# Spatial products of a gating group's two blocks, issued together in the down products' PSUM pool

## The chip, the cores and the metric

The kernel runs on one core of one Trainium2 chip. Its time is the device time of one execution in microseconds (us); the figure is the median of three runs. The core has five engines that work side by side, each on its own queue in order: TensorE (PE, matmuls; PEld is its weight load), VectorE (DVE), ScalarE (ACT), GpSimd (POOL, unused here) and SyncE (SP, which issues the DMAs). Matmul results land in PSUM banks, from which DVE and ACT read them. Engines wait for each other by semaphores.

## What is computed

One step of a two-layer streaming encoder for 1024 prompt frames and 32 sample frames, which share weights. Layer 0 has a spatial gating mixer (`sgu_mixer`), layer 1 a pooling mixer; each is followed by a squared-ReLU channel MLP, with RMSNorms and conditioning between. The part that the change touches is this:

```python
def sgu_mixer(h, w_in, g_v, w_s, b_s, w_out, T):
    z = jax.nn.gelu(h @ w_in)
    u, v = jnp.split(z, 2, axis=-1)
    v = rmsnorm(v, g_v)
    vr = v.reshape(bsz, L // T, T, SGU_GROUPS, SGU_GROUP_DIM)
    w = w_s[:, :T, :T] * sgu_chunk_mask()[:T, :T].astype(w_s.dtype)
    s = jnp.einsum('gij,bnjgd->bnigd', w, vr)
    s = s + jnp.transpose(b_s[:, :T])[None, None, :, :, None]
    s = s.reshape(bsz, L, D_SGU)
    return (u * s) @ w_out, v
```

The width is 1024, `u` and `v` are 2048 wide in 8 groups of 256, and T is 128 for the prompt and 32 for the sample.

## The kernel before

**Tiles and products.** The 1056 frames stand as columns in three tiles, `TILES` (L27): 384, 384, and 256 prompt plus 32 sample columns (288). Feature blocks of 128 stand on the partitions. A large product is done in three matmuls per weight block, as both operands are split into a high and a low fp32r part: `products` (L766) issues high·high (L771), high·low (L772) and low·high (L773). Splitting a weight costs one ACT copy (`wh`, L367) and one DVE subtraction (`wl`); splitting an activation costs the same two steps (`split`, ACT L925 and DVE). DVE instructions issued through the planner's wrappers all carry line L79 and are told apart by their tiles.

**The mixer's stages.** First `v` is computed for all frames and written to DRAM (`vd`). Then the loop at the end of the mixer runs over four pairs of groups, (0,1) to (6,7), and within a pair over the three tiles; each step is one `sgu_item`. An item has four blocks, two groups × two 128-wide halves k. For each block before the change `up(g, k)` does:
- if k is 0, `inputs(g)`: DMA of `vl` (the group's rows of `vd`, L968 and L973, on SP's queue) and DVE's scaling of the spatial weights by the frames' norms, `wr`;
- 24 matmuls into `pu`, and ACT's Gelu to `u` (L993);
- the spatial product `psp`: one plain fp32 matmul per 128-frame chunk (L997; each shows as two records), and a small one for the sample frames (L1005);
- DVE: s = psp·g_v + b, then s·u; `split` into `ush` and `usl`.

`down` then forms the item's share of `h = (u·s) @ w_out`: eight output blocks d, each 12 matmuls into `po` over the four pairs `ush`/`usl`, and adds each to the residual accumulator `acc` (ACT for the first pair of groups, DVE after that). `down` is put in `pending` and run by `flush()` of the next item, after that item's first `up`.

**Buffers.** PSUM has 8 banks, in three pools (L136 to L143): `pu` with 2, taken in turn by `ps_up`; `pd` with 3, by `ps_dn`; `pm` with 3, by `ps_ms`. SBUF work tiles come from tag "m" with 3 buffers (`t_m`: `u`, `s`, `wr`, some norm tiles) and tag "c" with 3 (`t_c`). A buffer's next user waits until its last user's readers are done.

**What sets the order.** The program is written out in order, and a planner adds work from other chains. `tick` (L69) advances a model time of PE, DVE calls advance a model time of DVE, and `weave` (L585) pulls a step from `fillers` (residual and modulation chains, conditioning products) whenever DVE's model time is behind PE's, each not before its `gates` time. The framework then fixes each engine's order at build from its own estimate. `weave` also takes steps of one stream of DRAM loads (issued on SP's queue into a few `raw` buffers, L359), which splits the weights and forms the conditioning products `ada` (L453) from DVE's sums `aa` of `w_ada`. In the mixer's first item these `ada` products stand among the matmuls, and a filler writes the sample state's rows: `vst` is loaded (L896), scaled on DVE and written out (L909), all on SP's queue, among which the `vl` loads stand. At the mixer's end, `to_ffn0` puts each tile's residual and modulation chain (`residual`, `modulate`: norms `pn`, `q`, `r`, eight `acc` updates, then `hh` on ACT and `hl` on DVE) into the fillers; the FFN's first products `pf` read `hh` and `hl` of tile 0.

Of the kernel before, what the change touches and what calls it, by code (L numbers as in the profile page):

```python
# [12 lines left out]
ALU = mybir.AluOpType  # L13
AX = mybir.AxisListType

P = 128
# [18 lines left out]
def tile_stream_encoder_step(  # L35
# [27 lines left out]
    mm = nc.tensor.matmul  # L63
# [5 lines left out]
    def tick(us):  # L69
        time["pe"] += us  # L70
        time["dve"] = max(time["dve"], time["pe"] - 4.0)

    def on_dve(op, fixed, rate):
        def run(out, *args, **kw):
            n = 1
            for k in out.shape[1:]:
                n *= k
            time["dve"] += fixed + n / rate
            return op(out, *args, **kw)  # L79

        return run

    tt = on_dve(nc.vector.tensor_tensor, 0.16, 930.0)
    stt = on_dve(nc.vector.scalar_tensor_tensor, 0.16, 840.0)
# [51 lines left out]
    def ps_up(name):  # L136
        return psum.tile([P, 512], F32, tag="pu", bufs=2, name=name)

    def ps_dn(name):
        return psum.tile([P, 512], F32, tag="pd", bufs=3, name=name)  # L140
# [4 lines left out]
    def t_m(name):  # L145
        return work.tile([P, 384], F32, tag="m", bufs=3, name=name)

    def t_c(name):
        return work.tile([P, 384], F32, tag="c", bufs=3, name=name)
# [4 lines left out]
    def t_x(name, shape):  # L154
        return work.tile(shape, F32, tag="x3", bufs=3, name=name)
# [16 lines left out]
    for i, parts in enumerate(rows):  # L172
        n = sum(k for _, k in parts)
# [25 lines left out]
    gvT = vecs[2][:, 24:40]  # L199
# [280 lines left out]
    def run_deferred():  # L480
        for _ in range(len(deferred)):
            deferred.pop(0)()
# [25 lines left out]
    def stream_ready():  # L508
        k = state["next"]
        if k >= len(stream):  # L510
            return False
        if stream[k][0] == "w":
            i = wpos[stream[k][1]] - W_SLOTS // 2
            return i < 0 or worder[i] in wdone
        return True

    def stream_step():

        k = state["next"]
        kind, key, ap, shape = stream[k]  # L520
        issue()
        run_deferred()
        r = raws.pop(k)
        if kind == "w":
            do_w(key, r)
        elif kind == "ada":
            (do_ada_pe if k < first_ada else do_ada)(*key, r)
        else:
            do_x(key, r)
        state["next"] += 1  # L530
        if in_raw(k):
            state["raw"] -= 1
        issue()
# [24 lines left out]
    def pull(force=False):  # L558

        def open_(f):
            return force or gates.get(f[0], 0.0) <= time["pe"]

        if sticky:
            f = sticky[-1]
            if not open_(f):
                return False
            sticky.pop()
        else:  # L570
            f = next((f for f in list(fillers)[:2] if open_(f)), None)
            if f is None:
                return False
        try:
            step = next(f[1])
        except StopIteration:
            fillers.remove(f)
            return True
        if step is True:
            sticky.append(f)  # L580
        elif step is not False:
            gates[f[0]] = max(time["pe"], time["dve"]) + step
        return True

    def weave(streams=1):  # L585
        if streams:
            n = 0
            run_deferred()
            while n < streams and stream_ready():
                stream_step()  # L590
                n += 1
        while time["dve"] < time["pe"] and fillers:
            if not pull():
                break
# [326 lines left out]
    def t_hid(kind, name):  # L921
        return work.tile([P, 384], F32R, tag="h" + kind, bufs=5, name=name)

    def split(dst_hi, dst_lo, src, n):
        act(out=dst_hi[:, :n], in_=src[:, :n], func=AF.Copy)  # L925
        tt(out=dst_lo[:, :n], in0=src[:, :n], in1=dst_hi[:, :n].bitcast(F32), op=ALU.subtract)
# [31 lines left out]
    def sgu_item(gs, t, mix, after):  # L958
        n = ncol[t]
        col0, npr, nsm = TILES[t]  # L960
        nch = npr // P
        hid = []
        vls, wrs = {}, {}

        def inputs(g):
            wt, _ = mix[g]
            vl = vls[g] = t_x(f"vl{g}_{t}", [P, 3, 256])
            nc.sync.dma_start(  # L968
                vl[:, :nch, :],
                vd[col0 : col0 + npr, g * 256 : (g + 1) * 256].rearrange("(c p) d -> p c d", p=P),  # L970
            )
            if nsm:
                nc.sync.dma_start(  # L973
                    vl[:nsm, nch, :], vd[SEQ : SEQ + nsm, g * 256 : (g + 1) * 256]
                )
            wr = wrs[g] = t_m(f"wr{g}_{t}")
            for c in range(nch):
                b = col0 // P + c
                ts(wr[:, c * P : (c + 1) * P], wt, rv[:, b : b + 1], None, op0=ALU.mult)
            if nsm:  # L980
                ts(wr[:nsm, npr : npr + nsm], wt[:nsm, :nsm], rv[:nsm, 8:9], None, op0=ALU.mult)

        def up(g, k):
            f = 2 * g + k
            if k == 0:
                inputs(g)
            vl, wr, bb = vls[g], wrs[g], mix[g][1]
            ps = ps_up(f"pu{g}_{t}_{k}")
            products(ps, n, up_terms(("u", g, k), t))
            if t == NT - 1:  # L990
                w_finish(("u", g, k))
            u = t_m(f"u{g}_{t}_{k}")
            act(out=u[:, :n], in_=ps[:, :n], func=AF.Gelu_apprx_tanh)  # L993
            sp = ps_up(f"psp{g}_{t}_{k}")
            tick(0.24 * nch + 0.2)
            for c in range(nch):
                mm(  # L997
                    sp[:, c * P : (c + 1) * P],
                    vl[:, c, k * P : (k + 1) * P],
                    wr[:, c * P : (c + 1) * P],  # L1000
                    start=True,
                    stop=True,
                )
            if nsm:
                mm(  # L1005
                    sp[:, npr : npr + nsm],
                    vl[:nsm, nch, k * P : (k + 1) * P],
                    wr[:nsm, npr : npr + nsm],
                    start=True,
                    stop=True,  # L1010
                )
            s = t_m(f"s{g}_{t}_{k}")
            stt(
                out=s[:, :npr].rearrange("p (c j) -> p c j", j=P),
                in0=sp[:, :npr].rearrange("p (c j) -> p c j", j=P),
                scalar=gvT[:, f : f + 1],
                in1=bb.unsqueeze(1).broadcast_to([P, nch, P]),
                op0=ALU.mult,
                op1=ALU.add,
            )  # L1020
            if nsm:
                stt(
                    out=s[:, npr : npr + nsm],
                    in0=sp[:, npr : npr + nsm],
                    scalar=gvT[:, f : f + 1],
                    in1=bb[:, :nsm],
                    op0=ALU.mult,
                    op1=ALU.add,
                )
            tt(out=s[:, :n], in0=s[:, :n], in1=u[:, :n], op=ALU.mult)  # L1030
            a, b = t_hid("h", f"ush{g}_{t}_{k}"), t_hid("l", f"usl{g}_{t}_{k}")
            split(a, b, s, n)
            hid.append((a, b))

        def down():
            for d in range(KB):
                ps = ps_dn(f"po{gs[0]}_{t}_{d}")
                terms = []
                for j, (a, b) in enumerate(hid):
                    wh, wl = need_w(("o", gs[j // 2], d // 4))  # L1040
                    o = (j % 2) * 512 + (d % 4) * P
                    terms.append((wh[:, o : o + P], wl[:, o : o + P], a[:, :n], b[:, :n]))
                products(ps, n, terms)
                accumulate(t, d, ps, gs[0] == 0)
                if d == 0 and after is not None:
                    st = Stat(t, f"rs_{t}")
                if after is not None:
                    st.square(d)
                if t == NT - 1 and d % 4 == 3:
                    for g in gs:  # L1050
                        w_finish(("o", g, d // 4))
                weave(d % 2)
            if after is not None:
                after(st)

        for j in range(4):
            up(gs[j // 2], j % 2)
            weave()
            if j == 0:
                flush()  # L1060
        pending.append(down)
# [102 lines left out]
    for gs in groups:  # L1164
        mix = {g: sgu_group(g) for g in gs}
# [281 lines left out]
```

## Time and profile before

| | |
|---|---|
| median of three runs | 2240.0 us (2239.03 to 2240.32) |
| profiled execution | 2238.69 us |
| its span in the profile | 2236.9 us |
| mean granted TensorE clock | 0.992 |
| mixer's items, from the first `pu` to the FFN's first `pf` | about 244 to 682 us |
| `pu` products | 384 matmuls of each kind, in 48 blocks |
| `psp` products | 48 blocks |

A profile row of the timeline reads: start, duration, engine, line, operation, out<-in, shape, count, and in brackets the idle time before it with what ended it. Matmuls are pipelined, so the pitch from one start to the next is what one costs, not its duration. A wait row reads: engine, tile and line, what it waited for, total us, times, longest. A row of a stretch gives busy time of PE, PEld, DVE, ACT and POOL with counts, then the granted clock, the DMA engines' share and GB/s.

### The profile page before, as it was taken

The page shows a single profiled execution, that of the slowest core. Times are in us where ns is not written, and L with a number is a line of the kernel's source. Part 1 is how long each engine was busy: PE and PEld are TensorE (multiplying, and loading weights), DVE is VectorE, ACT ScalarE, POOL GpSimd, SP SyncE. Part 2 cuts the span into 40 slices and gives each one's busy share as a digit, 9 for nine tenths or more (in the row PEclk, how much of TensorE's full clock was granted, in tenths as well). Part 3 has the DMA queues.
Part 4 walks back from the last instruction along what each step waited for, and adds up shares of the span by engine and source line. Part 5 has one row for each costly group of instructions (what it writes and reads, how often), then busy time and mean ns, then how long its engine had stood idle before and what let it go on. Part 6 is the DMA issues. An engine that isn't in the chain of part 4 may idle for free.

```text
span 2236.9 us, 33683 instructions
## 1 busy us (share of the span) xinstructions
PE 2197.3 (98%) x13478; PEld 2101.8 (94%) x13478; DVE 1371.4 (61%) x2609; ACT 957.5 (43%) x1645; POOL 0.7 (0%) x6
## 2 busy tenths in 40 slices
PE   7999799999999999999999999999999999999998
PEld 5777699999998999999999999999999999999998
DVE  4855735675568765766446869878765553424355
ACT  4633323121256654133435556666565542312334
POOL 0000000000000000000000000000000000000000
PEclk9999999999999999999999999999999999999998
DMA  8465613232235544333444546665454551202112
GB/s 298 149 226 164 206 53 116 79 126 88 78 104 184 171 132 142 104 123 109 132 125 131 166 156 201 184 189 163 145 166 135 152 155 45 93 10 85 57 50 95
DMA packets 344896, 295.67 MB, mean 132 GB/s; under 512 B 10178, under 2 KB 322954, under 8 KB 344740
## 3 DMA queue, kind: packets, MB, share of 16 engines
q1 hardware_dynamic: 344468, 293.43, 42.1%
q8 instruction: 105, 1.72, 0.3%
q14 instruction: 51, 0.42, 0.1%
q10 hardware_dynamic: 272, 0.10, 0.0%
HBM read 261.65 MB, written 31.84 MB: 131 GB/s over the span
## 4 chain that ended last, share of the span: by engine, by line
PE 91%; DMA 1%; DVE 1%; ACT 1%; issue 0%; DVEq 0%; SPq 0%; ACTq 0%
PE pf L771 11%; PE pf L772 11%; PE pf L773 11%; PE pg L771 11%; PE pg L772 11%; PE pg L773 11%; PE pu L771 3%; PE po L771 3%; PE po L772 3%; PE po L773 3%; PE pu L772 3%; PE pu L773 3%; PE pv L798 1%; PE pv L799 1%; PE pv L800 1%; PE pp L1310 1%
## 5 line engine op out<-in xcount | busy, mean ns | idle before, releaser
L771 PE MATMUL pf<-hh,wh_up 128*128 128x384 f32 (+1 forms) x1536 | 498.0, 324 | 1.2 <-ACT r L1075 1.0
L772 PE MATMUL pf<-hl,wh_up 128*128 128x384 f32 (+1 forms) x1536 | 497.0, 324 | 1.8 <-DVE hl L79 1.7
L771 PE MATMUL pg<-fh,wh_dn 128*128 128x384 f32 (+1 forms) x1536 | 498.3, 325 | 0.0
L773 PE MATMUL pf<-hh,wl_up 128*128 128x384 f32 (+1 forms) x1536 | 496.1, 323 | 0.0
L772 PE MATMUL pg<-fl,wh_dn 128*128 128x384 f32 (+1 forms) x1536 | 494.7, 322 | 0.0
L773 PE MATMUL pg<-fh,wl_dn 128*128 128x384 f32 (+1 forms) x1536 | 494.0, 322 | 0.0
L771 PEld LDWEIGHTS pf<-hh,wh_up 128*128 128x128 f32 x1536 | 288.6, 188 | 4.3 <-issue 2.0
L772 PEld LDWEIGHTS pf<-hl,wh_up 128*128 128x128 f32 x1536 | 288.7, 188 | 3.0 <-DVE hl L79 2.6
L771 PEld LDWEIGHTS pg<-fh,wh_dn 128*128 128x128 f32 x1536 | 288.4, 188 | 3.0 <-issue 1.2
L772 PEld LDWEIGHTS pg<-fl,wh_dn 128*128 128x128 f32 x1536 | 288.6, 188 | 0.7
L773 PEld LDWEIGHTS pg<-fh,wl_dn 128*128 128x128 f32 x1536 | 288.7, 188 | 0.0
L773 PEld LDWEIGHTS pf<-hh,wl_up 128*128 128x128 f32 x1536 | 288.6, 188 | 0.0
L367 ACT ACTIVATE wh_up<-raw 128x1024 fp32r<-128x1024 f32 x144 | 152.7, 1061 | 287.2 <-PE pf L772 230.8
L79 DVE TENSOR_TENSOR wl_up<-raw,wh_up 128x1024 fp32r<-128x1024 f32 x144 | 176.2, 1224 | 160.8 <-ACT wh_up L367 160.4
L79 DVE TENSOR_TENSOR acc<-acc,pg 128x384 f32<-128x384 f32 (+1 forms) x336 | 174.1, 519 | 159.8 <-PE pg L773 159.2
L367 ACT ACTIVATE wh_dn<-raw 128x1024 fp32r<-128x1024 f32 x144 | 152.7, 1061 | 206.2 <-PE pg L772 173.3
L79 DVE SCALAR_TENSOR_TENSOR aa<-raw,csil,aa 128x256 f32<-128x256 f32 x560 | 231.9, 478 | 2.4 <-DMA raw<-in_w_ada_dram 2.4
L79 DVE TENSOR_TENSOR wl_dn<-raw,wh_dn 128x1024 fp32r<-128x1024 f32 x144 | 176.2, 1224 | 86.4 <-ACT wh_dn L367 86.4
L1075 ACT ACTIVATE r<-pf 128x384 f32<-128x384 f32 (+1 forms) x192 | 86.6, 452 | 216.4 <-PE pf L773 211.6
L79 DVE TENSOR_TENSOR fl<-r,fh 128x384 fp32r<-128x384 f32 (+1 forms) x192 | 100.3, 523 | 115.0 <-ACT fh L925 113.6
L771 PE MATMUL pu<-hh,wh_u 128*128 128x384 f32 (+1 forms) x384 | 127.4, 332 | 0.9 <-DVE rv L874 0.9
L771 PE MATMUL po<-ush,wh_o 128*128 128x384 f32 (+1 forms) x384 | 125.6, 329 | 1.9 <-ACT ush L925 1.5
(254 smaller groups left out, 2904.2 us busy)
## 6 DMA issues: line engine op xcount, KB each, us to landing
raw<-in_ffn_w_up_dram SPq DMA_DIRECT2D x144, 512.0 KB, 4.1
raw<-in_ffn_w_down_dram SPq DMA_DIRECT2D x144, 512.0 KB, 3.4
raw<-in_w_ada_dram SPq DMA_DIRECT2D x96, 512.0 KB, 4.1
raw<-in_sgu_w_in_dram SPq DMA_DIRECT2D x32, 512.0 KB, 4.5
xd<-acc SPq DMA_DIRECT2D x8, 1536.0 KB, 7.4
xo_r<-xd SPq DMA_DIRECT2D x32, 384.0 KB, 3.7
vd<-vt SPq DMA_DIRECT2D x32, 256.0 KB, 2.9
raw<-in_sgu_w_out_dram SPq DMA_DIRECT2D x16, 512.0 KB, 3.8
```

The lines of the kernel that those rows point to most:

```text
L79: return op(out, *args, **kw)
L367: act(out=wh, in_=r, func=AF.Copy)
L771: mm(ps[:, :n], wh, rh, start=i == 0, stop=False)
L772: mm(ps[:, :n], wh, rl, start=False, stop=False)
L773: mm(ps[:, :n], wl, rh, start=False, stop=i == last)
L798: mm(ps[:m, :], a_h, wh[:, o : o + 512], start=k == 0, stop=False)
L799: mm(ps[:m, :], a_h, wl[:, o : o + 512], start=False, stop=False)
L800: mm(ps[:m, :], a_l, wh[:, o : o + 512], start=False, stop=k == KB - 1)
L1075: act(out=r[:, :n], in_=ps[:, :n], func=AF.Relu)
L1310: mm(ps[:, :n], wg[:, k, e * P : (e + 1) * P], A(t, 2 * g + k), start=k == 0, stop=k == 1)
```

## The change

`up` keeps the products and the Gelu and puts `u` in a list. A new `gate(g)`, called after the group's second `up`, issues the spatial products of both blocks behind one another into two banks of `pd`, then runs s, s·u and the split for both. `s` comes from tag "c" instead of "m", and one `tick(0.48 * nch + 0.2)` stands for two of `0.24 * nch + 0.2`. The number of matmuls and of DVE instructions is the same.

```diff
+        us = []
+
         def up(g, k):
-            f = 2 * g + k
             if k == 0:
                 inputs(g)
-            vl, wr, bb = vls[g], wrs[g], mix[g][1]
             ps = ps_up(f"pu{g}_{t}_{k}")
             products(ps, n, up_terms(("u", g, k), t))
             if t == NT - 1:
                 w_finish(("u", g, k))
             u = t_m(f"u{g}_{t}_{k}")
             act(out=u[:, :n], in_=ps[:, :n], func=AF.Gelu_apprx_tanh)
-            sp = ps_up(f"psp{g}_{t}_{k}")
-            tick(0.24 * nch + 0.2)
...
+            us.append(u)
+
+        def gate(g):
+
+            vl, wr, bb = vls[g], wrs[g], mix[g][1]
+            sps = []
+            tick(0.48 * nch + 0.2)
+            for k in range(2):
+                sp = ps_dn(f"psp{g}_{t}_{k}")
+                sps.append(sp)
+                for c in range(nch):
+                    mm(
+                        sp[:, c * P : (c + 1) * P],
+                        vl[:, c, k * P : (k + 1) * P],
+                        wr[:, c * P : (c + 1) * P],
+                        start=True,
+                        stop=True,
+                    )
...
+            for k, sp in enumerate(sps):
+                f = 2 * g + k
+                s = t_c(f"s{g}_{t}_{k}")
                 stt(
...
-            tt(out=s[:, :n], in0=s[:, :n], in1=u[:, :n], op=ALU.mult)
-            a, b = t_hid("h", f"ush{g}_{t}_{k}"), t_hid("l", f"usl{g}_{t}_{k}")
-            split(a, b, s, n)
-            hid.append((a, b))
+                tt(out=s[:, :n], in0=s[:, :n], in1=us.pop(0)[:, :n], op=ALU.mult)
+                a, b = t_hid("h", f"ush{g}_{t}_{k}"), t_hid("l", f"usl{g}_{t}_{k}")
+                split(a, b, s, n)
+                hid.append((a, b))
...
         for j in range(4):
             up(gs[j // 2], j % 2)
+            if j % 2 == 1:
+                gate(gs[j // 2])
             weave()
             if j == 0:
                 flush()
```

More of the change, by code (lines that the diff above doesn't have):

```diff
@@ L993, in up @@
             act(out=u[:, :n], in_=ps[:, :n], func=AF.Gelu_apprx_tanh)
-            sp = ps_up(f"psp{g}_{t}_{k}")
-            tick(0.24 * nch + 0.2)
[L996 to L1021, printed above, removed]
-                stt(
-                    out=s[:, npr : npr + nsm],
-                    in0=sp[:, npr : npr + nsm],
+            us.append(u)
@@ new lines, in gate @@
+        def gate(g):
[13 more added lines that the diff above has]
+                    )
+                if nsm:
+                    mm(
+                        sp[:, npr : npr + nsm],
+                        vl[:nsm, nch, k * P : (k + 1) * P],
+                        wr[:nsm, npr : npr + nsm],
+                        start=True,
+                        stop=True,
+                    )
+            for k, sp in enumerate(sps):
+                f = 2 * g + k
+                s = t_c(f"s{g}_{t}_{k}")
+                stt(
+                    out=s[:, :npr].rearrange("p (c j) -> p c j", j=P),
+                    in0=sp[:, :npr].rearrange("p (c j) -> p c j", j=P),
@@ L1025, in up @@
                     scalar=gvT[:, f : f + 1],
-                    in1=bb[:, :nsm],
+                    in1=bb.unsqueeze(1).broadcast_to([P, nch, P]),
                     op0=ALU.mult,
@@ L1029, in up @@
                 )
-            tt(out=s[:, :n], in0=s[:, :n], in1=u[:, :n], op=ALU.mult)
-            a, b = t_hid("h", f"ush{g}_{t}_{k}"), t_hid("l", f"usl{g}_{t}_{k}")
-            split(a, b, s, n)
-            hid.append((a, b))
+                if nsm:
+                    stt(
+                        out=s[:, npr : npr + nsm],
+                        in0=sp[:, npr : npr + nsm],
+                        scalar=gvT[:, f : f + 1],
+                        in1=bb[:, :nsm],
+                        op0=ALU.mult,
+                        op1=ALU.add,
+                    )
+                tt(out=s[:, :n], in0=s[:, :n], in1=us.pop(0)[:, :n], op=ALU.mult)
+                a, b = t_hid("h", f"ush{g}_{t}_{k}"), t_hid("l", f"usl{g}_{t}_{k}")
+                split(a, b, s, n)
+                hid.append((a, b))
         def down():
```

## The prediction

> **What bounds the kernel now.** I read the page's shares and chain first, then the busy time by stage, then TensorE's waits in the mixer, then the timeline around each wait.
>
> ```profile
> PE 2197.3 (98%) x13478; PEld 2101.8 (94%) x13478; DVE 1371.4 (61%) x2609; ACT 957.5 (43%) x1645; POOL 0.7 (0%) x6
> ...
> PE 91%; DMA 1%; DVE 1%; ACT 1%; issue 0%; DVEq 0%; SPq 0%; ACTq 0%
> ```
>
> TensorE (PE) is busy 98% of the span and is 91% of the chain that ended last. No matmul is added or taken away, so only idle time, half-clock time and switching cost of PE can change. The change touches the mixer, about 244 to 682 us. In the next rows the first columns are stretch, length, and busy PE; behind the counts stands the granted clock (0.97, 1.00, 0.99).
>
> ```profile
> 244.00:400.00 156.00, 144.76 (x913) 139.42 (x908) 88.82 (x210) 45.79 (x80) 0.00 (x0) 0.97 0.40 124
> 400.00:560.00 160.00, 160.00 (x1041) 155.67 (x1041) 98.81 (x236) 28.02 (x49) 0.00 (x0) 1.00 0.31 96
> 560.00:682.00 122.00, 119.40 (x752) 116.61 (x751) 76.91 (x151) 50.82 (x82) 0.00 (x0) 0.99 0.32 97
> ```
>
> PE lacks 11.2 us in the first stretch, nothing in the second, 2.6 us in the third. TensorE's waits over 240 to 690 us name the causes (total, times, longest):
>
> ```profile
> PE psp L997 <- DMA vl<-vd: 5.0, 1, 5.0
> PE ada L453 <- DVE aa L79: 4.6, 1, 4.6
> PE pf L772 <- DVE hl L79: 1.7, 1, 1.7
> PE po L771 <- ACT ush L925: 1.5, 1, 1.5
> ```
>
> Two single waits in the first item make 9.6 us; the others stand at the mixer's end. The steady middle has no wait of note except one that hides as pitch, next.
>
> **The change, part by part.** *(1) Gelu waits.* Tile `pu`'s answer lists, under idle time before its engine:
>
> ```profile
>   ACT u L993: 2.6, 16
> ```
>
> Two buffers of pool `pu` serve `pu` and `psp` in turn, so each `pu` takes the bank of the previous `pu` and waits for its Gelu. PE's timeline shows both kinds of block (start, duration):
>
> ```profile
> 280.88 0.83 PE L997 MATMUL psp<-wr,vl 128*128 128x128 f32 x6
> 281.68 0.44 PE L771 MATMUL pu<-hh,wh_u 128*128 128x384 f32 x1
> ...
> 285.95 0.83 PE L997 MATMUL psp<-wr,vl 128*128 128x128 f32 x6
> 286.53 0.42 PE L771 MATMUL po<-ush,wh_o 128*128 128x384 f32 x1
> 286.79 0.34 PE L772 MATMUL po<-usl,wh_o 128*128 128x384 f32 x1
> 286.96 0.34 PE L773 MATMUL po<-ush,wl_o 128*128 128x384 f32 x1
> ```
>
> From psp to the next product it is 0.80 us before `pu` and 0.58 us before `po`: 0.22 us of waiting, 16 times, 3.5 us; the list above says 2.6. After the change `psp` is in pool `pd`, `pu` alternates with `pu`, and the Gelu of two products ago was done 4 us before. I take 3.0 (2.6 to 3.5).
>
> *(2) Fewer switches.* A lone block of plain fp32 passes costs 0.58 for six passes of about 0.091 us (0.55), and the first matmul behind it holds 0.26 instead of the pitch of 0.17 (286.79 to 286.96): 0.12 us per block. The built program has 24 double blocks for 48 single ones: 24 × 0.12 = 2.8 us. Nothing hides it, since PE is the bound here. If the cost goes with passes and not with blocks, it is 0: I take 2.8 (0 to 2.9).
>
> *(3) The first item.* It is the largest term.
>
> ```profile
> 263.65 0.34 PE L773 MATMUL po<-ush,wl_o 128*128 128x384 f32 x1
> 268.59 1.04 PE L453 MATMUL ada<-aa,pick 128*32 128x128 f32 x8 [4.60 <-DVE aa L79]
> 274.60 1.62 PE L997 MATMUL psp<-wr,vl 128*128 128x128 f32 x6 [4.97 <-DMA vl<-vd]
> ...
> 266.98 0.33 SPq L909 DMA_DIRECT2D out_dram<-vst  x1
> ...
> 270.08 0.38 SPq L968 DMA_DIRECT2D vl<-vd  x1
> ```
>
> PE stops at `ada`, then at group 1's first `psp` until `vl` has landed, 4.5 us after its issue; `vl` stands in SP's queue behind the `vst` output, whose DMA it waits for (its place in that queue stays). In the built program three more `pu` products of 24 × 0.174 = 4.2 us now stand ahead of this pair of waits (group 1's second, and both that were behind the first `psp`), 12.5 us, and 18 `po` matmuls (3.1 us) fall behind it: 9.4 us more work ahead. The DVE instructions that feed `vst` and `aa` are moved too: I walked SP's and DVE's order by the rows' durations and get the issue of `vl` near 272 and its landing near 276.5, 1.9 us later. So 9.4 − 1.9 = 7.5 us less idle; about 1.5 us goes back, since the gate's result is then needed by the `po` matmuls close behind. I take 6.0. Lower bound 2: the queue is later by as much as the work ahead, bar the shorter stretch of half clock; upper bound 9: all 9.4 covered.
>
> *(4) The last item.* Rows of its waits, with start and end:
>
> ```profile
> 650.84 0.29 PE L771 MATMUL pu<-hh,wh_u 128*128 128x288 f32 x1
> ...
> 660.80 1.05 PE L997 MATMUL psp<-wr,vl 128*128 128x128 f32 x4 [0.58 <-DVE wr L79]
> ...
> 663.51 0.44 PE L772 MATMUL po<-usl,wh_o 128*128 128x288 f32 x1
> 663.75 0.44 PE L773 MATMUL po<-ush,wl_o 128*128 128x288 f32 x1
> ...
> 672.49 0.67 PE L771 MATMUL po<-ush,wh_o 128*128 128x288 f32 x3 [1.54 <-ACT ush L925]
> ...
> 682.28 0.34 PE L771 MATMUL pf<-hh,wh_up 128*128 128x384 f32 x1
> ```
>
> 650.84 to 682.28 is 31.4 us for 168 products at 0.131 (22.0), three psp blocks of 1.0 and four small matmuls (0.7): 25.7. So 5.7 us are lost, to 0.58, 1.54 and a half clock (pitch 0.24) in between. After, both `pu` of group 7 stand ahead of its `psp` (so `wr` is ready), and the two stalls become one at the second `ush`/`usl`; with DVE's order (s, s·u, a weight split of 1.2, usl, then the second block's) this comes 0.5 to 0.8 us late. Gain 4.9, less 0.7 for what the remaining gap may throttle: 4.2 (1 to 5).
>
> *(5) The boundary to the FFN: a loss.*
>
> ```profile
> 685.53 0.44 PE L772 MATMUL pf<-hl,wh_up 128*128 128x384 f32 x1 [1.69 <-DVE hl L79]
> ...
> 696.09 0.45 PE L771 MATMUL pf<-hh,wh_up 128*128 128x384 f32 x1 [1.01 <-ACT r L1075]
> ...
> 682.48 0.45 DVE L79 TENSOR_TENSOR acc<-acc,po 128x288 f32<-128x288 f32 x1 [0.35 <-PE po L773]
> ...
> 683.36 1.22 DVE L79 TENSOR_TENSOR wl_dn<-raw,wh_dn 128x1024 fp32r<-128x1024 f32 x1
> ...
> 689.53 0.61 DVE L79 SCALAR_TENSOR_TENSOR acc<-acc,coef,r_r_0x 128x384 f32<-128x384 f32 x1
> 690.06 0.61 DVE L79 SCALAR_TENSOR_TENSOR hl<-acc,mod,hh 128x384 fp32r<-128x384 f32 x1
> ...
> 692.79 0.61 DVE L79 SCALAR_TENSOR_TENSOR hl<-acc,mod,hh 128x384 fp32r<-128x384 f32 x1
> ```
>
> Before, tile 0's modulation (eight acc/hl pairs, alternating at 0.53) runs under the last `po`, so the FFN's first half starts at 682.28 and its second at 696.09, 13.8 us on, of which 48 matmuls at 0.174 are 8.4. In the built program the planner's changed estimate puts that chain behind tile 2's last sums on DVE and ScalarE, after the last `po`. From that `po`, E: acc 0.5, two wl_dn to 2.8, two sums and a scale to 4.7, q and r to 5.9, then sixteen instructions at 0.53 to about 15.0; PE, which follows hl by hl, begins the FFN's second half near E + 17.5. Loss 3.7 without half clock. PE's gaps there are short, but a short gap was followed by a throttled clock before:
>
> ```profile
> 660.00:666.40 6.40, 5.58 (x26) 4.71 (x25) 4.34 (x12) 6.00 (x9) 0.00 (x0) 0.75 0.27 89
> ```
>
> Here idle time of 0.8 us cost a mean clock of 0.75 over 6.4 us, that is 1.6 us at most. In the FFN much of that is hidden in waits for hl, so I add 0.8: −4.5 (−2 to −7, the upper loss with the full 1.6 us and each hl 0.1 us later).
>
> The Trainium skill, "TensorE: Matmul & The Clock Gate", section "HAM oscillation — how this bites in real kernels", gives the abstract rule that gaps matter above about 3.4 us. By that rule the short gaps of parts 4 and 5 would throttle nothing, and the sum would be 1.5 us larger. The row above speaks against it: a far shorter gap came with a clock of 0.75.
>
> *(6) The gate's result in the steady middle: 0.* The two blocks' s, s·u, ush, usl now come together, needed by the first `po` behind the next `pu`.
>
> ```profile
> 276.41 0.60 DVE L79 SCALAR_TENSOR_TENSOR s<-psp,vec,bs 128x384 f32<-128x384 f32 x1
> 277.12 0.56 DVE L79 TENSOR_TENSOR s<-s,u 128x384 f32<-128x384 f32 x1
> 278.27 0.56 DVE L79 TENSOR_TENSOR usl<-s,ush 128x384 fp32r<-128x384 f32 x1 [0.59 <-ACT ush L925]
> ...
> 272.85 3.63 DVE L79 SCALAR_TENSOR_TENSOR aa<-raw,csil,aa 128x256 f32<-128x256 f32 x9
> ```
>
> Six instructions of about 0.5 us and one ScalarE hop: 3.4 us after the gate with DVE free. The cover is 24 `pu` products (4.2 us) and six `po` products of the first group (1.0): 5.2 us, 1.8 spare; one weight split of 1.2 fits. DVE is busy 98.8 of 160 us in this stage, so it holds most times. The waits of the two `psp` on sums of earlier `po` in pool `pd` are covered by the same `pu`. The two ticks made one and `s` in another pool cost no instruction; their effect is the order used above.
>
> **Sum.** −3.0 − 2.8 − 6.0 − 4.2 + 4.5 = −11.5 us. The profiled execution took 2238.69 us (span 2236.9 and 1.8 around it); the runs' median, 2240.0, is 1.3 above it, so I take the change off the median: 2228.5.
>
> **The rivals.** *(a) The first item's wait only moves.* If `vl` and `aa` are later by as much as the work put ahead (DVE is the feeder of both, and `aa` rows of 3.63 us stand in its way), term 3 is 0 to 1 and the sum −5.5: 2234.5. For it: `vl`'s place in the queue is unchanged. Against: DVE has less than 2 us more to do ahead of it.
>
> *(b) Slower: the gate's burst comes late on DVE in most items.* Point of decision: more than 1.8 us of other DVE work ahead of the burst. The `aa` row of 3.63 us would do it: 1.8 us late, in 11 items 20 us, less the 11.5 and with no gain at the tail: about +12, 2252. With one item in two it is break-even near 2239. Against: no `po` wait on usl is seen in the middle of the mixer before, and a single split does not exceed the spare time.
>
> *(c) No change.* The chain at the boundary costs 7 and the first item gives its lower bound of 2, with parts 2 and 4 halfway down: −3.0 − 1.5 − 2.0 − 2.5 + 7.0 = −2.0, 2238. The wait of 1.69 on hl shows that DVE is the feeder there; against it, my walk gives 3.7.
>
> That the change fails to do what it says I hold for out: the built order has both `psp` blocks behind the second `pu` in all 24 gates.
>
> **How the numbers follow.** Forecast 0.53, (a) 0.17, (b) 0.15, (c) 0.15. A measurement of this kernel tells 0.2%, 4.5 us, from no change. Faster: nearly all of the forecast (its own range, from the terms' ends taken together in part, is 2221 to 2237, so 0.49), two thirds of (a), 0.12, and a little of (b)'s milder end, 0.03: 0.64. Within: 0.04 + 0.05 + 0.13 + 0.01: 0.22. Slower: 0.14. The range runs from 2220 (first item at 9, tail at 5) to 2245, which takes in (a), (c) and the break-even side of (b).
>
> **What would show it.** In the changed profile: no idle time ahead of `pu` that ends with the Gelu; psp blocks twice as long and half as many; one wait on `vl` under 4 us instead of 5.0, and `ada`'s 4.6 gone; the last item near 26.5 us from `pu` of group 6's second block; FFN's second half 17 to 19 us after the last `po` instead of 13.8, with waits on hl. Wrong would be: waits of `po` on usl all through 300 to 650 us (rival b), or a first-item stall still near 9 us (rival a).

## The result, and the profile after

| | before | changed |
|---|---|---|
| median of five runs | 2239.65 us (2238.24 to 2240.32) | 2230.30 us (2227.71 to 2231.41) |
| profiled execution | 2238.69 us | 2227.71 us |
| span in the profile | 2236.9 us | 2225.9 us |

The ratio is 0.9958, 95% interval 0.9945 to 0.9971: 9.4 us faster, where 11.5 us were forecast (2228.5, range 2220 to 2245).

TensorE's waits of the changed kernel, 240 to 700 us (total, times, longest), answer to those of before:

```profile
PE pn_rs L671 <- ACT sc_rs L656: 3.8, 1, 3.8
PE psp L1005 <- DMA vl<-vd: 2.7, 1, 2.7
PE pf L771 <- ACT hh L745: 1.8, 1, 1.8
PE wsT L952 <- DMA ws<-in_sgu_w_s_dram: 1.6, 2, 1.1
```

The wait of 4.6 us on `aa` is gone, the one on `vl` is 2.7 for 5.0, and neither `pu` on `rv` nor `po` on `ush` is left. New are 3.8 us of `pn_rs` and 1.8 of `pf` on `hh`, both behind the mixer's last `po`. Between 300 and 640 us only one wait stands, of 1.1 us on `ws`, so the gate's burst on DVE is covered in the steady middle.

Before the mixer nothing is changed, yet the two profiles are 2 us apart there. So the stretches are counted from the last `ada` block ahead of the mixer's first `pu` to the FFN's first `pg`. PE's timeline, before:

```profile
243.85 0.42 PE L453 MATMUL ada<-aa,pick 128*32 128x128 f32 x8
...
708.92 0.34 PE L771 MATMUL pg<-fh,wh_dn 128*128 128x384 f32 x1
```

and after:

```profile
245.84 0.42 PE L453 MATMUL ada<-aa,pick 128*32 128x128 f32 x8
...
697.57 0.34 PE L771 MATMUL pg<-fh,wh_dn 128*128 128x384 f32 x1
```

That is 465.1 us before and 451.7 after, 13.3 us less in this pair; the rest of the span behind it is 1528.0 and 1528.3. The two profiled executions are 11.0 us apart, because the time ahead of the mark is 2.0 us longer in the changed kernel's. That execution is also the fastest of its five, so 13.3 us is at the high end. The same stretch in a second profile of the changed kernel is 452.7. The time ahead of the mark lies between 242.6 and 246.6 us over the profiles of this study, which is why single spans are poor evidence for a microsecond or two here.

**The first item, after.** PE's timeline at the stall, then SP's:

```profile
273.60 0.34 PE L773 MATMUL pu<-hh,wl_u 128*128 128x384 f32 x1
273.87 0.43 PE L453 MATMUL ada<-aa,pick 128*32 128x128 f32 x8
277.03 1.58 PE L1005 MATMUL psp<-wr,vl 128*128 128x128 f32 x12 [2.73 <-DMA vl<-vd]
278.36 0.42 PE L771 MATMUL po<-ush,wh_o 128*128 128x384 f32 x1
```

```profile
269.46 0.33 SPq L909 DMA_DIRECT2D out_dram<-vst  x1
...
272.23 0.38 SPq L359 DMA_DIRECT2D raw<-in_w_ada_dram  x1
272.67 0.50 SPq L968 DMA_DIRECT2D vl<-vd  x1
```

Four `pu` now run ahead of `ada`, which finds `aa` ready. `vl` lands 277.03 − 245.84 = 31.2 us after the mark (before: 274.60 − 243.85 = 30.8). Until then PE has three `pu` more to do (12.5 us) and 18 `po` less (3.1 us), so 9.4 us more work. `vl` is issued right behind a load of `w_ada` that stands ahead of it in SP's queue and that had waited 1.9 us for DVE's sums `aa`.

Six `pu` and the first item's 96 `po` are done when the next `psp` starts, before:

```profile
304.33 0.83 PE L997 MATMUL psp<-wr,vl 128*128 128x128 f32 x6
```

and after:

```profile
295.27 1.50 PE L1005 MATMUL psp<-wr,vl 128*128 128x128 f32 x12
```

From the mark that is 60.5 us before and 49.4 after.

**The last item and the boundary, after.**

```profile
639.76 0.29 PE L771 MATMUL pu<-hh,wh_u 128*128 128x288 f32 x1
...
667.10 0.29 PE L773 MATMUL po<-ush,wl_o 128*128 128x288 f32 x1
671.14 0.61 PE L671 MATMUL pn_rs<-sc_rs,ones 128*128 128x288 f32 x1 [3.75 <-ACT sc_rs L656]
671.69 0.61 PE L671 MATMUL pn_rs<-sm_rs,ones 128*128 128x288 f32 x1
674.05 0.69 PE L771 MATMUL pf<-hh,wh_up 128*128 128x384 f32 x1 [1.75 <-ACT hh L745]
...
684.98 0.45 PE L771 MATMUL pf<-hh,wh_up 128*128 128x384 f32 x1 [0.29 <-ACT r L1087]
```

From group 6's second `pu` to the last `po`'s end (667.23) are 27.5 us, one psp block of about 0.9 more than before, against 31.4: 4.9 us gained. The FFN's second half starts 17.75 us after that, against 13.8: 3.9 us lost. DVE shows what came late there:

```profile
667.42 0.45 DVE L79 TENSOR_TENSOR acc<-acc,po 128x288 f32<-128x288 f32 x1 [0.16 <-PE po L773]
667.79 2.35 DVE L79 TENSOR_TENSOR wl_dn<-raw,wh_dn 128x1024 fp32r<-128x1024 f32 x2
670.07 0.45 DVE L79 TENSOR_TENSOR sq_rs<-sq_rs 128x288 f32<-128x288 f32 x1
671.12 0.52 DVE L79 SCALAR_TENSOR_TENSOR sm_rs<-sq_rs,eps,sc_rs 128x288 fp32r<-128x288 f32 x1 [0.60 <-ACT sc_rs L656]
671.55 0.55 DVE L79 SCALAR_TENSOR_TENSOR q_r_0x<-pn_r_0x,q_r_0x 128x384 f32<-128x384 f32 x1
```

Tile 0's chain begins with `q_r_0x` at 671.55, behind the last `po`. Before, it began with 10 us of `po` still to run (to 682.28):

```profile
671.91 0.56 DVE L79 SCALAR_TENSOR_TENSOR q_r_0x<-pn_r_0x,q_r_0x 128x384 f32<-128x384 f32 x1
```

### The profile page after: what moved, and what is told of

It is laid out like the page before. It is cut to its first block, busy times and chain, and to the rows that moved or that the text cites. A ratio compares the mean times of both kernels' runs of the same rounds, so it can differ in the third digit from the quotient of the medians.

```text
span 2225.9 us, 33634 instructions
## 1 busy us (share of the span) xinstructions
PE 2191.3 (98%) x13478; PEld 2096.9 (94%) x13478; DVE 1370.2 (62%) x2609; ACT 950.1 (43%) x1641; POOL 0.7 (0%) x6
## 4 chain that ended last, share of the span: by engine, by line
PE 86%; DMA 1%; ACT 0%; DVE 0%; issue 0%; DVEq 0%; SPq 0%; ACTq 0%
PE pf L771 11%; PE pf L772 11%; PE pf L773 11%; PE pg L771 11%; PE pg L772 11%; PE pg L773 11%; PE po L771 3%; PE po L772 3%; PE po L773 3%; PE pu L771 2%; PE pu L773 2%; PE pu L772 2%; PE psp L1005 1%; PE pp L1322 1%; PE ada L453 0%; PE yT L1405 0%
## 5 line engine op out<-in xcount | busy, mean ns | idle before, releaser
L773 PE MATMUL pu<-hh,wl_u 128*128 128x384 f32 (+1 forms) x384 | 124.5, 324 | 0.0
```

Source lines behind the costliest of these rows:

```text
L773: mm(ps[:, :n], wl, rh, start=False, stop=i == last)
```

## The experiments

Each median is set against runs of the kernel before on the same chip (2239.6 to 2239.8 us). "The stretch" is the one from the mark to the first `pg`; before it is 465.1 us.

**1. The changed kernel again.** No edit.

> The changed kernel once more, as the mark for the other three. Theory A (most of the gain is the first item: work moved ahead of the two waits for aa and vl; the rest is the Gelu waits and the last item, less 4 us at the boundary to the FFN): about 2229 us, one wait on vl of 2 to 4 us, none on aa, and from the first pu of the mixer to the FFN's second half about 439 us as in the first profile (678.7 to 684.98 less 245.84), whatever the 0 to 244 us before it do. Theory B (the gain is bank separation and fewer blocks, all through the mixer): the same time, so this run tells nothing between them.

Measured 2229.18 us, ratio 0.9951 (0.9938 to 0.9963), stretch 452.7, wait on `vl` 3.0. The stretch is within 1 us of the first profile's.

**2. All items but the first gated together.** In `sgu_item`, with the old body kept as `up_old`:

```diff
+        together = not (gs[0] == 0 and t == 0)
         for j in range(4):
-            up(gs[j // 2], j % 2)
-            if j % 2 == 1:
-                gate(gs[j // 2])
+            if together:
+                up(gs[j // 2], j % 2)
+                if j % 2 == 1:
+                    gate(gs[j // 2])
+            else:
+                up_old(gs[j // 2], j % 2)
```

> The changed kernel, with the old order in the very first item only (groups 0 and 1, first tile); the other 11 items are gated together. Theory A: 8 to 10 us slower than the changed kernel, about 2238, with the waits of 4.6 us on aa and 5.0 us on vl back. Theory B: one item of 12 is undone, so at most 1 us slower, about 2230.

Measured 2239.0 us, ratio 0.9999 (0.9991 to 1.0008): 9.8 us slower than the changed kernel beside it, and the gain is gone. Its waits, same columns as above:

```profile
PE psp L1059 <- DMA vl<-vd: 5.0, 1, 5.0
PE ada L453 <- DVE aa L79: 4.6, 1, 4.6
PE pn_rs L671 <- ACT sc_rs L656: 3.8, 1, 3.8
PE pf L771 <- ACT hh L745: 1.8, 1, 1.8
```

Theory A's number. What the other 11 items give (stretch 463.1, 2.0 less than before) is small, because the last item's gain is paid back at the boundary.

**3. Only the first item gated together, and 4. only the first two.**

```diff
+        together = gs[0] == 0 and t == 0     # 3
+        together = gs[0] == 0 and t < 2      # 4
```

> The old kernel, with both blocks gated together in the first item only. Theory A: 8 to 10 us faster than before, about 2230, since the first item's waits are shortened and the boundary to the FFN keeps its old order (no loss of 4 us), while the Gelu waits (about 3 us) and the last item's 5 us stay. Theory B: at most 1 us faster, about 2239.

> The old kernel, with both blocks gated together in the first two items (groups 0 and 1, first and second tile). The first item alone gave 4.8 us, with waits of 2.0 us on aa and 4.7 us on vl: only the one pu that the next item has free in the old order stood ahead of the stall. Theory A (vl lands about 31 us after the mixer's start whatever is changed, and the gain is the work that stands ahead of it): with the second item gated too its second pu comes ahead as well, the waits become about 0 on aa and 2.7 on vl as in the changed kernel, and the time is 4 to 5 us below that of the first item alone: 2230. Theory B (the gain is spread over the gates): one gate pair more, under 1 us: 2234.

Measured 2234.82 us (ratio 0.9978, 0.9970 to 0.9987) and 2230.05 us (0.9958, 0.9945 to 0.9970). The first number was a miss: half of what was expected. The waits say why. In the third:

```profile
PE psp L1005 <- DMA vl<-vd: 4.7, 1, 4.7
PE ada L453 <- DVE aa L79: 2.0, 1, 2.0
```

and in the fourth:

```profile
PE psp L1005 <- DMA vl<-vd: 2.9, 1, 2.9
```

With the old order in the second item its second `pu` must wait for its first `psp`, which stands behind the stall; so three `pu` cover it and not four. Gating the second item adds the fourth (4.2 us), and the time falls by 4.8. Two items of twelve then give as much as the whole change. Part of that equality is a chance of sums: they have no loss at the boundary, and neither the last item's gain.

**5. The old order with psp in the down products' pool.**

```diff
-            sp = ps_up(f"psp{g}_{t}_{k}")
+            sp = ps_dn(f"psp{g}_{t}_{k}")
```

> The old order, block by block, with psp's bank from the down products' pool instead of the up products' pool. Theory A: only the Gelu waits go: psp to the next pu takes 0.58 us instead of 0.80 in 16 places, 3.5 us, about 2236; the first item's waits of 4.6 and 5.0 us stay. Theory B: most of the gain, about 2231. Theory C (psp now waits for sums of earlier po in that pool): no gain or slower, 2240 or more, with waits of psp on acc.

Measured 2228.64 us, ratio 0.9948 (0.9935 to 0.9962): theory A's number missed, theory B's held. PE's timeline in the middle, and at the first item:

```profile
305.00 0.83 PE L997 MATMUL psp<-wr,vl 128*128 128x128 f32 x6
305.58 0.42 PE L771 MATMUL pu<-hh,wh_u 128*128 128x384 f32 x1
```

```profile
267.98 0.81 PE L453 MATMUL ada<-aa,pick 128*32 128x128 f32 x8 [1.11 <-DVE aa L79]
274.55 2.90 PE L997 MATMUL psp<-wr,vl 128*128 128x128 f32 x12 [5.76 <-DMA vl<-vd]
```

psp to `pu` is 0.58 us, as expected of the Gelu waits. What I had not seen: with the up banks free of `psp`, the framework puts three `pu` ahead of the stall, with no order written for it. `ada` waits 1.1 us instead of 4.6, `vl` still 5.8. The stretch is 453.7: its first item gains about 3.4 us (to the point where six `pu` and the item's 96 `po` are done, 57.5 us, with an `ada` block of 0.4 more in it, against 60.5), its last item and the middle the rest, and its boundary does not lose (25.2 us from the last `po` to `pg`, against 26.6 before and 30.3 after the change). From the end of the first item to group 6's second `pu` in the last tile, which is the steady middle, PE takes 346.5 us before, 342.5 here (with an `ada` block of 0.4 less) and 344.5 in the changed kernel. So one word of the diff gives the whole gain; as against this kernel the grouping adds some 7 us in the first item and 2 in the last, and takes 5 back at the boundary and about 1.6 in the middle.

**6. The grouping in the up products' pool.**

```diff
-                sp = ps_dn(f"psp{g}_{t}_{k}")
+                sp = ps_up(f"psp{g}_{t}_{k}")
```

> Both blocks' spatial products together as in the changed kernel, but in the two banks of the up products' pool. Theory A (free up banks are what lets the next pu run on, past the Gelu and past the first item's stall): psp waits for both Gelus and the next pu for the sums s; 0.5 to 1 us in each of 24 gates and the first item's stall back; 2245 to 2260. Theory D (the order alone does it): about 2230.

Measured 2244.39 us, ratio 1.0025 (1.0016 to 1.0034): slower than before, by a little less than theory A had it. A double block ahead of an `ada` takes 1.66 us, where the changed kernel's takes 1.43:

```profile
301.00 1.74 PE L1005 MATMUL psp<-wr,vl 128*128 128x128 f32 x12
302.66 0.41 PE L453 MATMUL ada<-aa,pick 128*32 128x128 f32 x2
```

and the first item waits 2.9 on `aa` and 4.4 on `vl`. Counted as in experiment 5, the order alone gains about 3 us in the first item and about 3 in the last (each with one `psp` block of work taken out of the comparison); it loses 5.0 in the middle, where `pu` and `psp` now wait for `s` and for the Gelu, and 4.9 at the boundary. The order alone does not pay; the free up banks are what makes the difference between this kernel and the changed one.

**7. The two blocks' chunks in turn.**

```diff
-            for k in range(2):
-                sp = ps_dn(f"psp{g}_{t}_{k}")
-                sps.append(sp)
-                for c in range(nch):
+            sps = [ps_dn(f"psp{g}_{t}_{k}") for k in range(2)]
+            for c in range(nch):
+                for k, sp in enumerate(sps):
...
+            for k, sp in enumerate(sps):
                 if nsm:
```

> The changed kernel, with the chunks of the two psp blocks in turn, so that each fp32 product goes to the other bank than the one before. A double block takes 1.26 us until the next pu, 0.58 and 0.68: if the extra 0.1 us is the price of changing the bank, 1.26 becomes about 1.7 (five changes instead of one), and the kernel 24 x 0.4 = 10 us slower than the changed one, about 2239. If it is the start of a run of products behind a wait, 1.26 stays and so does the time, about 2229.

Measured 2229.05 us, ratio 0.9950 (0.9936 to 0.9963), as the changed kernel (2229.18). The double block of a tile of 384 columns takes 1.25 or 1.26 us in 12 of 16 cases, as in the changed kernel: five bank changes cost no more than one, so the extra 0.1 us of a second block is not the bank's price. The rows say what it is. The changed kernel's first double block:

```profile
255.47 1.50 PE L1005 MATMUL psp<-wr,vl 128*128 128x128 f32 x12
256.73 0.42 PE L771 MATMUL pu<-hh,wh_u 128*128 128x384 f32 x1
256.99 0.34 PE L772 MATMUL pu<-hl,wh_u 128*128 128x384 f32 x1
```

A row of six passes lasts 0.83 us (the lone blocks in the prediction), one of eight 1.05 (below), one of twelve 1.50: each further pass adds 0.11 us. Twelve passes at 0.111 and one product at 0.174 make 1.51, and from 255.47 to 256.99 it is 1.52. For the lone block, six passes and one product make 0.84, and from 285.95 to 286.79 it is 0.84. So both kinds of block cost their passes and nothing besides; the next matmul's row merely starts 0.09 us early.

In the third tile the double block is shorter. First the changed kernel, then this one:

```profile
643.49 0.40 PE L1013 MATMUL psp<-wr,vl 32*128 32x32 f32 x2
643.83 0.71 PE L1005 MATMUL psp<-wr,vl 128*128 128x128 f32 x4
644.47 0.40 PE L1013 MATMUL psp<-wr,vl 32*128 32x32 f32 x2
644.80 0.40 PE L771 MATMUL pu<-hh,wh_u 128*128 128x288 f32 x1
```

```profile
642.54 1.05 PE L1004 MATMUL psp<-wr,vl 128*128 128x128 f32 x8
643.52 0.63 PE L1013 MATMUL psp<-wr,vl 32*128 32x32 f32 x4
644.08 0.40 PE L771 MATMUL pu<-hh,wh_u 128*128 128x288 f32 x1
```

1.54 us for 1.84 (642.96 to 644.80): the small products stand together, and one change between the two forms is left of three. Eight such blocks should save 2.4 us, which the time does not show: the wait on `vl` is 3.1 us here and a clock of 0.64 follows it (last section), so the end of the first item comes 51.5 us after the mark, where it is 49.4 and 50.3 in the two profiles of the changed kernel.

**8. Group 1's vl fetched with group 0's, in the first item.**

```diff
+            if gs[0] == 0 and t == 0:
+                if g == 0:
+                    fetch(0)
+                    fetch(1)
+            else:
+                fetch(g)
```

(`fetch` is the DMA part of `inputs`.)

> The changed kernel, with the DMA of group 1's vl issued right behind group 0's in the first item, ahead of the sample state's rows; nothing else moved. Theory A (after the change vl still lands about 31 us after the mixer's start, as before it, since its buffer comes free with the state rows' chain; what the change did is to put 12.5 us of pu in front): the wait of 2.7 to 3.0 us on vl goes, the next limit is ada's wait on aa, 0 to 2 us; 1 to 3 us faster than the changed kernel, about 2227. Theory B (vl's transfer itself is slow or the DMA queues are full there): the wait stays, 2229.

Measured 2224.65 us, ratio 0.9928 (0.9914 to 0.9941), 4.5 us below the changed kernel of experiment 1, a little above the range expected. The wait on `vl` is gone. The transfer itself had not been what was slow: the changed kernel's `vl` loads from 235 to 300 us take 3.1 to 4.2 us from issue to landing, this kernel's 2.7 to 6.2. What was late was the issue. Which of its two conditions held it, the buffer or the load of `w_ada` ahead of it in the queue, this run does not separate: in the first profile the load did, in the second the last 0.5 us was a wait for the `vst` output. `ada`'s wait on `aa` does not return, but that is no test of it, since in this build the block stands behind the item's `po`.

**9. Tile 0's chain woven into the last down products.** In `down`, behind `weave(d % 2)`:

```diff
+                if after is not None and t == NT - 1:
+                    for _ in range(2):
+                        if any(f[0] == "ffn0_0" for f in fillers):
+                            pull(True)
```

> The changed kernel, with two steps of tile 0's residual and modulation chain forced into each output block of the mixer's last down products. Theory A: the boundary's loss goes and more: the FFN's second half starts some 9 to 10 us after the last po instead of 17.8, no waits of pn on sc_rs (3.8) and of pf on hh (1.8); 6 to 9 us faster than the changed kernel, 2221 to 2223. If DVE is short there too (16 instructions of 0.53 us more among the po sums), po waits on acc for 2 to 4 us and the gain is 3 to 5: 2225.

Measured 2225.04 us, ratio 0.9929 (0.9917 to 0.9942): 4.1 us below experiment 1, under the range of 6 to 9. It is the number of the lower case, but not for the reason named with it: no `po` waits on `acc`. One wait is left at the boundary:

```profile
679.07 0.40 PE L671 MATMUL pn_rs<-sc_rs,ones 128*128 128x288 f32 x1 [2.48 <-ACT sc_rs L656]
```

Tile 2's norm matmul stands in PE's queue among the first `pf` and holds them up. The chain is the cause of the wait on `hh`, and the norm matmul a second stop of its own.

**10. Experiments 8 and 9 together, and 11. with two more edits:** the chunks in turn (7), and a later norm for the last tile:

```diff
-            yield 1.2
+            yield 9.0 if self.tag == f"rs_{NT - 1}" else 1.2
```

> The changed kernel with both single edits: group 1's vl issued early in the first item (4.5 us by itself) and tile 0's chain woven into the last down products (4.1 us by itself). If they are two separate places, the gains add: 2220 to 2221. If the boundary takes back what the first item gives, 2224.

> Both edits, and two more: the norm matmul of the last tile is not pulled before 9 us of the planner's time have passed (its wait of 2.5 us on sc_rs stood in PE's queue ahead of the FFN's products), and the spatial chunks are issued in turn over the two blocks (in the third tile a double block took 1.54 us instead of 1.84, in the others 1.26 as before). If these are real: 2.5 and 8 x 0.3 = 2.4 us less, 2215 to 2217. If PE only waits elsewhere at the boundary, 2219 to 2220.

Measured 2220.73 us (ratio 0.9916, 0.9903 to 0.9930) and 2217.95 us (0.9904, 0.9891 to 0.9918). The two places add. The last two edits bring 2.8 us of 4.9 expected: the wait of the norm matmul went only from 2.5 to 2.1 us, and the rest is about what the chunks were to save (2.4). The last kernel is faster than both: 21.6 us below the kernel before, where the change has 9.4.

## Why the prediction was right or wrong

The forecast of 11.5 us held for the time (9.4 by the medians, 13.3 by the stretch in the first pair of profiles and 12.4 with the second profile of the changed kernel). That the sum came so close is in part luck: part 2 gave nothing where 2.8 were counted, and part 3 gave about 4 more than counted.

1. *Gelu waits, 3.0.* Right. In experiment 5, which changes nothing else about a block, psp to `pu` is 0.58 us where it was 0.80, and its middle is 3.6 us shorter with the `ada` block set aside; experiment 6 shows the waits come back in the up pool. In the changed kernel no idle time ahead of `pu` ends with the Gelu.
2. *Fewer switches, 2.8.* Wrong: 0, its lower bound. The step that failed is "six passes of about 0.091 us (0.55)", and with it "0.12 us per block". A pass costs 0.111 us (7), so six cost 0.67; 0.55 us is five steps, from the first start to the last. With 0.111, the 0.58 us of a lone block and the 0.09 by which the next matmul holds longer are the passes themselves, and no price of a switch is left to be saved. It is the case that the prediction named, that the cost goes with passes and not with blocks. In the middle the double blocks even lose about 1.6 us against the single ones of experiment 5.
3. *First item, 6.0.* Mechanism right (2, 3, 4 and 8), size too small, and beyond its upper bound of 9: to the point where six `pu` and the first item's 96 `po` are done, before took 60.5 us from the mark and after 49.4, which is one psp block less of work; about 10 us are gained. The step that was mis-sized is the working of `vl`: its landing moved by 0.4 us (1.5 in the second profile), not 1.9, and nothing "goes back" behind the gate. The waits on `aa` and `vl` fell from 9.6 to 2.7. Two things were not in the term. About 1.4 us comes from the clock: behind the stall `psp` had taken 1.27 us instead of 0.58 and `pu` 5.0 instead of 4.3, and in the changed kernel's first profile the clock there is 1.00. Another 0.9 is the wait of the second `pu` on `rv` (0.87 us at 251.37 before), which neither the changed kernel nor experiments 5 and 6 have.
4. *Last item, 4.2.* Measured 4.9. `psp` finds `wr` ready, as worked out. The one late stall of 0.5 to 0.8 us that was to be left is not among the waits, and the clock from 640 to 667 us is 1.00.
5. *Boundary, −4.5.* Measured −3.9: FFN's second half at E + 17.75 for 17.5. That the sum agrees is partly luck, for the rows that PE stops at are other ones: not hl by hl, but `pn_rs` on `sc_rs` (3.8) and then the first `hh` (1.8). I had counted tile 2's sums on DVE and not the norm matmul that they feed, which stands ahead of `pf` in PE's queue. Behind them the granted clock is 0.51 from 674 to 678 us, up to 2.0 us where 0.8 were counted, and no wait on `hl` is left. The chain was late in any case, so the sum hardly changes; for the repair it matters (9). The loss stands in every kernel here whose last items are gated together (also 2, 6, 7 and 8) unless the chain is woven in, and in none with the old order there (3, 4 and 5). Whether it is the order or the planner's time, which a gate moves on by 0.2 less than two old blocks did, is not shown.
6. *Steady middle, 0.* Right for the waits: the only one of 300 to 640 us is on `ws`. Rival (b) is out.

From the end of the first item's `po` to the last item PE gains only 2.0 us, where the shares of parts 1 and 2 that fall there had come to about 5; part 2's zero explains 2.4 of the missing 3. A slip without effect: the four chances of "within" add up to 0.23, not 0.22. Rival (a) is refuted by the wait on `vl`, and (c) by the sizes of 3 and 5.

What the prediction did not ask is whether the grouping is needed at all. Its part 1 took the banks for a matter of 0.22 us waits. Experiments 5 and 6 show that they count in part 3 too. With the old order in both, three `pu` run ahead of the stall in experiment 5 and one before; with the grouping in both, four in the changed kernel and two in experiment 6. A `pu` can only be put ahead of a stalled `psp` if it has a bank.

## What to carry to other kernels

When two products share a small rotating PSUM pool, ask not only what each waits for in the steady state but what the scheduler could run ahead at a stall if the pool were free; moving one of them to another pool may be the whole gain. Measure the stretch between two marks in the trace where runs differ by microseconds ahead of the change. Before you price a switch, find what one pass costs by setting rows of different length side by side; a cost that grows in step with the passes is no switch.

## What was not expected of the hardware

**The same wait is followed by a full or a halved clock.** The wait on `vl` is 2.73 us in the changed kernel and 3.02 in its second profile, 2.94 with two items gated together (4), 3.13 with the chunks in turn (7). The 4 us behind it, in this order (busy PE behind the length; the granted clock behind the counts):

```profile
277.00:281.00 4.00, 3.97 (x27) 3.83 (x28) 4.00 (x11) 1.04 (x3) 0.00 (x0) 1.00 0.87 277
```

```profile
277.00:281.00 4.00, 3.97 (x27) 4.00 (x28) 4.00 (x11) 1.24 (x4) 0.00 (x0) 1.00 0.80 248
```

```profile
277.00:281.00 4.00, 3.97 (x18) 4.00 (x19) 3.00 (x8) 0.08 (x1) 0.00 (x0) 0.57 0.82 262
```

```profile
277.40:281.40 4.00, 3.95 (x19) 3.98 (x20) 3.25 (x8) 0.00 (x0) 0.00 (x0) 0.64 0.80 258
```

Clock 1.00 and 1.00, then 0.57 and 0.64, so 2.94 us cost up to 1.7 us more where 3.02 cost none. The gap's length alone does not decide. The Trainium skill, "TensorE: Matmul & The Clock Gate", section "🔬 Part 1: The HAM clock gate (the "warmup" mystery)", says that the activity window of about 3.4 us is free-running, so that the point of transition depends on where in the window the work lands. These four rows agree with that, though the profile does not show where the window lies, and so does the short gap near 660 us that had gone with a clock of 0.75. The rule of thumb in the prediction, that only gaps above about 3.4 us matter, is not borne out by them.

**The time ahead of the mixer varies by 4 us** (242.6 to 246.6 at the mark) among the profiles of this study, whose kernels differ only behind it; two profiles of the changed kernel itself are 1.0 us apart (244.82 and 245.84).
